# Feed-forward part of a two-block network: the up projection by seven products for eight, the convolution added up in PSUM, the output projection by halves of the tokens

## The chip, the core and the metric

The kernel runs on one core of a Trainium2 chip. The metric is device time in microseconds (us) from the first to the last instruction; a smaller one is better. The engines named below are TensorE (PE in the profile), VectorE (DVE), ScalarE (ACT), GpSimd (POOL) and SyncE (SP, which issues most of the loads and stores). Each works through its own instructions in order; a semaphore holds an instruction, and all behind it on its engine, until what it needs is there.

## What is computed

Two blocks in a row on 1024 tokens of 1024 features. The first (gated linear attention and pooled differences) is not touched. Of the second, cut to what matters:

```python
def second_block(x, ...):
    h = rmsnorm_2(x, attn_norm_g)
    ...                                   # o_fox, o_sb: two kinds of attention, 8 heads each
    o = concatenate([rmsnorm_2(o_fox, fox_out_g), rmsnorm_2(o_sb, sb_out_g)])   # 512 + 512 features
    x = x + o @ w_out                     # output projection, 1024 x 1024
    h = rmsnorm_2(x, ffn_norm_g)
    u = causal_dwconv(h @ w_up, conv_w, conv_b)   # w_up: 1024 x 5632; 3 taps over the tokens, per feature
    gate, val = split(u, 2)               # 2816 features each: 22 tiles of 128
    x = x + (silu(gate) * val) @ w_down   # w_down: 2816 x 1024
    return rmsnorm_2(x, final_norm_g)
```

All is float32 to the caller. A product is made of three float32r matmuls (`mm3`): each operand is split into a high and a low part, and hi·lo, lo·hi and hi·hi are added up in PSUM.

## The kernel before

Activations lie with the features on the 128 partitions and the tokens along the row: `x2` is eight tiles of 128 x 1024. A bank of PSUM holds 128 x 512 values, so each tile of a product's output takes two banks, one for each half of the tokens (`XH`). A weight tile of 128 x 512 (four blocks of 128 features by 128 columns) comes through `load`: one load from memory (256 KB, issued by SP), a cast to the high part on ACT (`whi`), a subtraction for the low part on POOL (`wlo`). There are two buffers for raw weights and four for each part. `tt` (L182) and `stt` (L185) are the helpers for two-operand and scaled two-operand arithmetic, on VectorE unless POOL is named; `split` casts at L190, or at L193 with a scale.

Between the attention and the end, the steps are:

- **Output projection, second half** (from L1105). `out_fox` has made x = xr + (fox half of o) @ w_out while the attention ran (its last additions, `x<-x,t`, are on POOL). What is left is the half of `o_sb`: 8 column tiles (ct) x 2 halves of tokens x 4 features tiles x 3 = 192 matmuls. `gemm_late` takes the first three column tiles: 54 matmuls with the feature tiles 4 to 6, then the norm of `o_sb` (`bank_rstd` at L272, then `rstd`: a multiply-add, Ln, Exp and three more VectorE steps), then the 18 with feature tile 7. The compiler's scheduler, which orders what is ready by priority, puts the 54 between the last steps of the attention. Each result is t = bank * rs, x += t; then the square of x on ACT, its sum `acc` on POOL, and the two parts `u3h`, `u3l` of x * ffg.
- **Up projection.** Column tile 0 is begun by `gemm_late` with the first six feature tiles, before the norm R3 is known. `conv` makes one of the 44 column tiles (22 of gates, 22 of values): 48 matmuls, the two banks times R3, the first tap by ACT (Identity with scale and bias), two taps by `stt`. `up_group` makes two gate and two value tiles, sigmoid and two multiplications, and splits the result into `fh`, `fl` (POOL).
- **Down projection.** After each `up_group`, `down` multiplies the group before by its weights: 11 groups x 96 matmuls, each bank added to `x2`, which stays on the chip. The last group and the final norm go by ranges of tokens (`SEQ`).

PE's matmuls of the feed-forward part: 44 x 48 = 2112 up and 11 x 96 = 1056 down.

## Time and profile before

| | us |
|---|---|
| time, three executions | 2674.43, 2674.55, 2679.32 (median 2674.55) |
| time of the profiled execution | 2679.32 (its span: 2679.3) |
| TensorE busy in the span | 2549.1 (95%) |
| VectorE, ScalarE, GpSimd busy | 1505.9, 961.0, 809.5 |
| from the norm of `o_sb` (1868.2) to the first up matmuls without a gap (1930.5) | 62.3 |
| up and down projections without a gap (1930.5 to 2609.3) | 678.8 |
| the rest, with the last down products and the final norm (2609.3 to 2679.3) | 70.0 |

The profiled execution is the slowest of the three, 4.8 us above the median. Times in the rows count from the start of the span. A row of a stretch gives its length, then the busy time (and the count of instructions) of PE, PEld, DVE, ACT and POOL, the clock that TensorE was granted (1.00 is 2.4 GHz), the share of the DMA engines and GB/s. In a row of the timeline the first number is the start, the second the busy time from there, and the brackets hold the idle time ahead of it with what ended it; `x4` means that neighbours were put together.

### The profile page before, as it was taken

How to read it: one execution, taken by the hardware profiler on the slowest of the kernel's cores; microseconds unless marked ns; L12 is line 12 of the kernel's file. 1: busy time of each engine (PE TensorE's matmuls, PEld its weight loads, DVE VectorE, ACT ScalarE, POOL GpSimd, SP SyncE). 2: the span in 40 equal slices, each digit the busy share in tenths (PEclk: the TensorE clock that was granted, in tenths of full speed). 3: DMA queues.
4: the chain of work that ended last, by engine and by line, in shares of the span. 5: the costliest groups of instructions: out<-in, count | busy, mean ns of one | idle time of the engine just before them, and what ended most of it. 6: DMA issues, size and time to landing. Idle time of an engine off the chain costs nothing. (4 is left out here: it accounts for less than half of the span.)

```text
span 2679.3 us, 36279 instructions
## 1 busy us (share of the span) xinstructions
PE 2549.1 (95%) x14390; PEld 2015.2 (75%) x14390; DVE 1505.9 (56%) x2190; ACT 961.0 (36%) x1634; POOL 809.5 (30%) x592
## 2 busy tenths in 40 slices
PE   6989999999999999999999999999899999999996
PEld 3878977777787888876777766666688888888885
DVE  6363292765927223255766677788934444444456
ACT  4342262553734412332333443433422222222233
POOL 1432221221212224434233222233433333333334
PEclk9989999999999999999999999999999999999998
DMA  6423242433424553335444323430111111111112
GB/s 256 125 74 108 86 158 85 151 111 101 145 80 146 196 193 110 118 103 155 127 127 127 113 77 114 124 105 28 40 49 49 48 48 48 47 48 48 48 48 75
DMA packets 109113, 270.55 MB, mean 101 GB/s; under 512 B 13600, under 2 KB 18592, under 8 KB 108944
## 3 DMA queue, kind: packets, MB, share of 16 engines
q1 hardware_dynamic: 101648, 244.90, 28.3%
q0 software_dynamic: 7296, 23.34, 3.7%
q8 instruction: 113, 1.85, 0.3%
q14 instruction: 56, 0.46, 0.1%
HBM read 192.40 MB, written 71.57 MB: 99 GB/s over the span
## 5 line engine op out<-in xcount | busy, mean ns | idle before, releaser
L182 POOL TENSOR_TENSOR wlo<-wraw,whi 128x512 fp32r<-128x512 f32 (+1 forms) x363 | 537.3, 1482 | 1639.2 <-ACT whi L190 1593.1
L190 ACT CAST whi<-wraw 128x512 fp32r<-128x512 f32 (+1 forms) x363 | 223.8, 617 | 709.4 <-PE pp L238 617.6
L236 PE MATMUL pp<-hl,whi 128*128 128x512 f32 (+1 forms) x768 | 312.1, 407 | 4.8 <-DVE hl L185 4.8
L237 PE MATMUL pp<-hh,wlo 128*128 128x512 f32 (+1 forms) x768 | 307.2, 400 | 0.4 <-POOL wlo L182 0.4
L238 PE MATMUL pp<-hh,whi 128*128 128x512 f32 (+1 forms) x768 | 306.4, 399 | 0.0
L238 PE MATMUL pp<-u3h,whi 128*128 128x512 f32 x688 | 271.4, 395 | 0.0
L237 PE MATMUL pp<-u3h,wlo 128*128 128x512 f32 x688 | 271.0, 394 | 0.0
L236 PE MATMUL pp<-u3l,whi 128*128 128x512 f32 x688 | 270.2, 393 | 0.0
L182 DVE TENSOR_TENSOR x<-x,pp 128x512 f32<-128x512 f32 (+1 forms) x184 | 121.5, 664 | 208.5 <-PE pp L238 208.5
L236 PEld LDWEIGHTS pp<-hl,whi 128*128 128x128 f32 (+1 forms) x768 | 144.9, 189 | 42.5 <-DVE hl L185 5.8
L237 PEld LDWEIGHTS pp<-hh,wlo 128*128 128x128 f32 (+1 forms) x768 | 144.8, 189 | 38.9 <-issue 6.1
L238 PEld LDWEIGHTS pp<-hh,whi 128*128 128x128 f32 (+1 forms) x768 | 144.9, 189 | 33.7 <-issue 0.4
L1028 DVE COPY pt<-pg 128x512 f32<-128x512 f32 (+2 forms) x192 | 101.0, 553 | 92.5 <-PE pg L1026 91.8
L237 PEld LDWEIGHTS pp<-u3h,wlo 128*128 128x128 f32 x688 | 129.0, 188 | 30.9
L236 PEld LDWEIGHTS pp<-u3l,whi 128*128 128x128 f32 x688 | 129.2, 188 | 30.3
L238 PEld LDWEIGHTS pp<-u3h,whi 128*128 128x128 f32 x688 | 129.1, 188 | 30.1
L236 PE MATMUL pp<-fl,whi 128*128 128x512 f32 (+1 forms) x368 | 142.0, 386 | 0.0
L238 PE MATMUL pp<-fh,whi 128*128 128x512 f32 (+1 forms) x368 | 141.4, 384 | 0.0
L237 PE MATMUL pp<-fh,wlo 128*128 128x512 f32 (+1 forms) x368 | 140.8, 383 | 0.0
L185 DVE SCALAR_TENSOR_TENSOR t<-p,vec,t 128x1023 f32<-128x1023 f32 x88 | 122.1, 1395 | 33.1 <-ACT t L1144 32.1
L237 PE MATMUL pp<-uh,wlo 128*128 128x512 f32 x336 | 139.2, 414 | 0.0
L236 PE MATMUL pp<-ul,whi 128*128 128x512 f32 x336 | 138.3, 412 | 0.0
(384 smaller groups left out, 5434.0 us busy)
## 6 DMA issues: line engine op xcount, KB each, us to landing
wraw<-in_w_up SPq DMA_DIRECT2D x88, 256.0 KB
wraw<-in_w_qk SPq DMA_DIRECT2D x48, 256.0 KB
wm<-in_w_mod SPq DMA_DIRECT2D x24, 512.0 KB
wraw<-in_w_dn SPq DMA_DIRECT2D x44, 256.0 KB
x<-in_xT SPq DMA_DIRECT2D x16, 512.0 KB
wraw<-in_w_v SPq DMA_DIRECT2D x32, 256.0 KB
wraw<-in_w_out SPq DMA_DIRECT2D x32, 256.0 KB
q<-qs_d POOLq DMA_DIRECT2D x16, 512.0 KB, 5.0
```

The costliest lines, as they stand in the source:

```text
L182: return (eng or nc.vector).tensor_tensor(out=o, in0=a, in1=b, op=op)
L185: return (eng or nc.vector).scalar_tensor_tensor(out=o, in0=a, scalar=s, in1=b, op0=op0, op1=op1)
L190: nc.scalar.copy(hi, src)
L236: nc.tensor.matmul(ps, ah, bl, start=first, stop=False)
L237: nc.tensor.matmul(ps, al, bh, start=False, stop=False)
L238: nc.tensor.matmul(ps, ah, bh, start=False, stop=last)
L1028: nc.vector.tensor_copy(o, ps[:, :w])
```

## The change

Line numbers after the change are 8 to 20 higher (`tt` L190, `stt` L193, `split`'s cast L199, loads and stores L202, `mm3` L254 to L256).

1. From the output projection to the end of the up projection every instruction is kept in the program's order on its engine (`pinned`).
2. The output projection goes by halves of the tokens, A = 512 to 1023 first, then B = 0 to 511. Each half of x is written to memory (`x2_d`) and read back before the down projection.
3. The up projection takes seven products in place of eight. With w = [[a11, a12], [a21, a22]] for a gate tile and a value tile (rows: the pair (gate, value); columns: the two halves of the features), and the four quarters of h = x * ffg * R3 (two halves of the features, two of the tokens), seven sums of weights meet seven sums of quarters: 22 pairs x 7 products x 4 x 3 = 1848 matmuls. `t_norm` scales a quarter, `t_sum` forms a sum of quarters in place of x, `t_parts` splits it into the 28 tiles `T`; `up_sum` forms four sums of weights per pair on VectorE; `up_parts` splits seven weights per pair. `up_result` puts the products together: two copies on ACT, the other sums on VectorE.
4. The convolution's first tap goes to PSUM (`cv`), and the two others are added there; the sigmoid and the multiplication read it there. The gated result is stored (`f_d`).
5. The down projection runs after the whole up projection, from memory (`gated`), with its 1056 matmuls and the same last part.

```diff
+SEVEN = (1, 6, 2, 5, 7, 3, 4)
+EARLY = (1, 2, 5, 7, 6, 3, 4)
...
-    rs["sb"] = b1k("rs")
-    first = gemm_late(
-        [[load(io["w_out2"][ct, 1], 4, P)] for ct in range(3)], oh, ol, range(4, 8), TAGS[:3], 3,
-        lambda: bank_rstd(acc_o["sb"], rs["sb"], 1.0 / 512, "pg"),
-    )
...
+    get = psum_pool(es, pp=(HALF, 4), cv=(L, 2))
+    pinned[0] = True
...
+    def out_result(ct, half, ps):
+        x, t = x2[ct][:, half], ht("t")
+        tt(t, ps, rs["sb"][:, half], ALU.mult)
+        tt(x, x, t, ALU.add)
+        dma(x2_d[ct][:, half], x)
...
+    def t_norm(k, half):
+        x = quarter(k, half)
+        stt(x, x, V("ffg", k), R3[:, half], ALU.mult, ALU.mult)
+    def t_sum(n, j):
+        o, a, b = {
+            5: ((j, A), (j, B), (j, A)), 7: ((j, B), (j + 4, B), (j, B)),
+            6: ((j + 4, B), (j + 4, B), (j, A)), 4: ((j + 4, A), (j + 4, A), (j + 4, B)),
+        }[n]
+        tt(quarter(*o), quarter(*a), quarter(*b), ALU.subtract)
+    def t_parts(n, j):
+        src = quarter(*{1: (j, A), 2: (j + 4, A), 3: (j + 4, B), 5: (j, A), 7: (j, B), 6: (j + 4, B), 4: (j + 4, A)}[n])
+        t = b1k("T", F32R)
+        split(src, t[:, :HALF], t[:, HALF:], nc.gpsimd if j % 2 else None)
+        T[n].append((t[:, :HALF], t[:, HALF:]))
...
+    def up_sum(q, n):
+        if q >= NFF or (q, n) in sums:
+            return
+        a11, a12, a21, a22 = raws[q]
+        if n in (5, 6):
+            r = ctile("S")
+            sums[q, 5], sums[q, 6] = r[:, :HALF], r[:, HALF:]
+            tt(sums[q, 5], a21, a22, ALU.add)
+            tt(sums[q, 6], sums[q, 5], a11, ALU.subtract)
+        elif n == 3:
+            sums[q, 3] = sums[q, 6]
+            tt(sums[q, 3], a12, sums[q, 6], ALU.subtract)
+        elif n == 7:
+            tt(a11, a11, a21, ALU.subtract)
+            sums[q, 7] = a11
+        else:
+            sums[q, n] = raws[q][{1: 0, 2: 1, 4: 3}[n]]
...
+    def up_product(q, n):
+        wh, wl = wparts.pop((q, n))
+        key = {1: 1, 2: 1, 7: 7, 4: 7}.get(n, 6)
+        new = (q, key) not in banks
+        if new:
+            banks[q, key] = get("pp")
+        ps = banks[q, n] = banks[q, key]
+        for j in range(4):
+            th, tl = T[n][j]
+            mm3(ps, wh[:, j], wl[:, j], th, tl, new and j == 0, j == 3, True)
...
+    def up_result(q, n):
+        b = banks[q, n]
+        p1, u = part.get((q, 1)), part.get((q, "u"))
+        if n == 1:
+            part[q, 1] = ht("p1")
+            copy(part[q, 1], b)
+        elif n == 2:
+            copy(out_row(q, 0)[:, A], b)
+        elif n == 3:
+            tt(out_row(q, 0)[:, B], p1, b, ALU.add)
+        elif n == 4:
+            tt(out_row(q, 1)[:, A], u, b, ALU.add)
+        elif q > 1 and n == 6:
+            part[q, "u"] = ht("u")
+            tt(part[q, "u"], p1, b, ALU.add)
+        elif q > 1 and n == 5:
+            tt(out_row(q, 1)[:, B], p1, b, ALU.add)
+        elif n == 5:
+            part[q, "u"] = ht("u")
+            copy(part[q, "u"], b)
+        elif n == 6:
+            v = out_row(q, 1)[:, B]
+            tt(v, p1, b, ALU.add)
+            tt(u, v, u, ALU.subtract)
+            tt(v, v, banks[q, 7], ALU.add)
+        elif q > 1:
+            v = out_row(q, 1)[:, B]
+            tt(v, v, b, ALU.add)
...
+    def up_rest(q, i):
+        if i == 0:
+            conv_first(q, 0)
+        elif i == 1:
+            conv_first(q, 1)
+            conv_tap(q, 0, 1)
+        elif i == 2:
+            conv_tap(q, 0, 2)
+        elif i == 3:
+            g = act(outs[q, 0], cv[q, 0], AF.Sigmoid)
+            if q == NFF - 1:
+                log_exp_table(g)
+            conv_tap(q, 1, 1)
+        elif i == 4:
+            conv_tap(q, 1, 2)
+        elif i == 5:
+            tt(outs[q, 0], outs[q, 0], cv[q, 0], ALU.mult)
+        else:
+            tt(outs[q, 0], outs[q, 0], cv[q, 1], ALU.mult)
+            dma(f_d[q], outs[q, 0])
...
+    three = [out_load(ct) for ct in range(3)]
+    wide = get("cv")
+    bank3 = [[get("pp"), get("pp")], [get("pp"), get("pp")], [wide[:, :HALF], wide[:, HALF:]]]
+    for w, bs in zip(three, bank3):
+        for b, half in zip(bs, (A, B)):
+            out_product(b, w, half, range(3))
+    wide = get("cv")
+    for half in (A, B):
+        half_rstd(acc_o["sb"], half, wide[:, half], rs["sb"], 1.0 / 512)
+    for i, half in enumerate((A, B)):
+        for ct in range(3):
+            out_product(bank3[ct][i], three[ct], half, (3,))
+    for i, half in enumerate((A, B)):
+        for ct in range(3):
+            out_result(ct, half, bank3[ct][i])
+    todo = [(ct, half) for half in (A, B) for ct in range(3, KD)]
+    ws = [out_load(ct) for ct, _ in todo[:2]]
+    total = None
+    for n, (ct, half) in enumerate(todo):
+        ps = get("pp")
+        out_product(ps, ws[n], half, range(4))
+        if n + 2 < len(todo):
+            ws.append(out_load(todo[n + 2][0]))
+        out_result(ct, half, ps)
+        if n == 4:
+            total = get("cv")
+            half_rstd(acc, A, total[:, A], R3, 1.0 / D)
+            for q in range(2):
+                up_load(q)
+        elif n > 5:
+            for k in (2 * (n - 6), 2 * (n - 6) + 1):
+                t_norm(k, A)
+                t_parts(1 + k // 4, k % 4)
+    order = [(q, n) for n in EARLY for q in range(2)] + [(q, n) for q in range(2, NFF) for n in SEVEN]
+    for q, n in order[:3]:
+        up_parts(q, n)
+    prep = {
+        1: [(t_norm, j, B) for j in range(4)] + [(t_sum, 5, j) for j in range(4)], 2: [(t_parts, 5, j) for j in range(4)],
+        3: [(t_norm, j + 4, B) for j in range(4)] + [(t_sum, 7, j) for j in range(4)], 4: [(t_parts, 7, j) for j in range(4)],
+        5: [(t_parts, 3, j) for j in range(4)], 6: [f for j in range(4) for f in ((t_sum, 6, j), (t_parts, 6, j))],
+        7: [f for j in range(2) for f in ((t_sum, 4, j), (t_parts, 4, j))],
+        8: [f for j in range(2, 4) for f in ((t_sum, 4, j), (t_parts, 4, j))],
+    }
+    for s, (q, n) in enumerate(order):
+        i = s % 7
+        if s == 1:
+            half_rstd(acc, B, total[:, B], R3, 1.0 / D)
+        if s:
+            up_result(*order[s - 1])
+        for f, *a in prep.get(s, ()):
+            f(*a)
+        if s == 8:
+            up_load(2)
+        elif q > 1 and i == 0 and q + 1 < NFF:
+            up_load(q + 1)
+        if i == 3 and s > 7:
+            up_sum(q + 1 if q > 1 else 2, 6)
+        if s + 4 < len(order):
+            up_sum(*order[s + 4])
+        if s + 3 < len(order):
+            up_parts(*order[s + 3])
+        if q > 2:
+            up_rest(q - 1, i)
+        elif s >= 13:
+            for i_ in ((0, 1), (2, 3), (4, 5), (6,))[(s - 13) % 4]:
+                up_rest((s - 13) // 4, i_)
+        up_product(q, n)
+    up_result(*order[-1])
+    for i in range(7):
+        up_rest(NFF - 1, i)
+    pinned[0] = False
...
+    def gated(grp):
+        return unzip([load_split(f_d[2 * grp + kk], lo=nc.gpsimd) for kk in range(2)])
...
-    f = up_group(0)
+    f = gated(0)
+    for ct in range(KD):
+        x2[ct] = b1k("x2")
+        nc.sync.dma_start(x2[ct], x2_d[ct])
     for grp in range(NFF // 2 - 1):
-        nf = up_group(grp + 1)
+        nf = gated(grp + 1)
         for c2 in range(4):
             down(grp, load_down(grp, c2), c2, *f)
```

What the change moves, at three places (rows in the order in which they stand on an engine; `out<-in` with the buffers' numbers; `_16193` and the like are numbers, `pp`, `lg`, `pg`, `cv` banks of PSUM).

**TensorE and GpSimd, end of the attention.** `ol`, `oh` are the parts of `o_sb`, `sm` and `pt` the attention's weights, `whi`, `wlo` the parts of a weight tile. TensorE before:

```order
L952 MATMUL lg_16120<-k_2815_15498,q_2814_15497 128x256
L953 MATMUL lg_16120<-k_2816_15499,q_2814_15497 128x256
L236 MATMUL pp_16209<-ol_14098,whi_16192 128x512
L237 MATMUL pp_16209<-oh_14097,wlo_16193 128x512
L238 MATMUL pp_16209<-oh_14097,whi_16192 128x512
L236 MATMUL pp_16209<-ol_14777,whi_16192 128x512
L237 MATMUL pp_16209<-oh_14776,wlo_16193 128x512
L238 MATMUL pp_16209<-oh_14776,whi_16192 128x512
L236 MATMUL pp_16209<-ol_15491,whi_16192 128x512
L237 MATMUL pp_16209<-oh_15490,wlo_16193 128x512
L238 MATMUL pp_16209<-oh_15490,whi_16192 128x512
L236 MATMUL lg_16211<-ol_14098,whi_16198 128x512
```

TensorE after:

```order
L1057 MATMUL pg_16085<-pt_16078,vt_15524 64x128 x2
L1046 MATMUL pg_16147<-ident,sm_16141 128x128
L1046 MATMUL pg_16161<-ident,sm_16155 128x128 x2
L1057 MATMUL pg_16165<-pt_16146,vt_15524 64x128
L1057 MATMUL pg_16165<-pt_16160,vt_15524 64x128 x2
L254 MATMUL pp_16246<-ol_14128,whi_16228 128x512
L255 MATMUL pp_16246<-oh_14127,wlo_16229 128x512
L256 MATMUL pp_16246<-oh_14127,whi_16228 128x512
```

GpSimd before, at the same place:

```order
L182 TENSOR_TENSOR wlo_16205<-wraw_16203,whi_16204 128x512
L182 TENSOR_TENSOR x_2916_15942<-x_2916_15942,t_15943 128x512 x2
L182 TENSOR_TENSOR wlo_16345<-wraw_16343,whi_16344 128x512
L182 TENSOR_TENSOR x_2943_16066<-x_2943_16066,t_16067 128x512 x2
L182 TENSOR_TENSOR x_2965_16149<-x_2965_16149,t_16150 128x512 x2
L182 TENSOR_TENSOR wlo_16389<-wraw_16387,whi_16388 128x512
```

GpSimd after:

```order
L190 TENSOR_TENSOR x_2916_15972<-x_2916_15972,t_15973 128x512 x2
L190 TENSOR_TENSOR x_2943_16096<-x_2943_16096,t_16097 128x512 x2
L190 TENSOR_TENSOR x_2965_16179<-x_2965_16179,t_16180 128x512 x2
L190 TENSOR_TENSOR wlo_16229<-wraw_16227,whi_16228 128x512
L190 TENSOR_TENSOR wlo_16235<-wraw_16233,whi_16234 128x512
L190 TENSOR_TENSOR wlo_16241<-wraw_16239,whi_16240 128x512
```

The first 54 matmuls of the output projection no longer stand between the attention's steps but behind the last of them (`pg<-pt,vt`), and the low parts of their weights stand behind all additions `x<-x,t` of `out_fox`.

**SyncE, output projection.** `wraw<-in_w_out` is a load of weights, `xr` a load of the residual, `x_d<-x` a store of half a tile of x. Before:

```order
L231 DMA wraw_16197<-in_w_out 128x512
L231 DMA wraw_16203<-in_w_out 128x512
L1089 DMA xr_15941<-x_d_173 128x1024
L231 DMA wraw_16343<-in_w_out 128x512
L1089 DMA xr_16065<-x_d_174 128x1024
L231 DMA wraw_16387<-in_w_out 128x512
L1089 DMA xr_16148<-x_d_175 128x1024
L231 DMA wraw_16431<-in_w_out 128x512
L231 DMA wraw_16475<-in_w_out 128x512
```

After:

```order
L202 DMA wraw_16227<-in_w_out 128x512
L202 DMA wraw_16233<-in_w_out 128x512
L202 DMA wraw_16239<-in_w_out 128x512
L202 DMA x_d_176<-x_2764_15298 128x512
L202 DMA x_d_177<-x_2794_15431 128x512
L202 DMA x_d_178<-x_2829_15570 128x512
L202 DMA x_d_176<-x_2764_15298 128x512
L202 DMA x_d_177<-x_2794_15431 128x512
L202 DMA x_d_178<-x_2829_15570 128x512
L202 DMA wraw_16379<-in_w_out 128x512
L202 DMA wraw_16385<-in_w_out 128x512
```

The fourth and all later loads of weights stand behind the six stores of x, each of which waits for its result.

**VectorE, start of the up projection.** Before, the results of a column tile (`p` is a bank times R3, `t` the convolved tile):

```order
L182 TENSOR_TENSOR p_17323<-pp_17337,R_3051_16562 128x512
L182 TENSOR_TENSOR p_17323<-pp_17363,R_3051_16562 128x512
L185 SCALAR_TENSOR_TENSOR t_17324<-p_17323,vec,t_17324 128x1023
L185 SCALAR_TENSOR_TENSOR t_17324<-p_17323,vec,t_17324 128x1022
L182 TENSOR_TENSOR p_17392<-pp_17406,R_3051_16562 128x512
L182 TENSOR_TENSOR t_17324<-t_17324,sgf_17461 128x1024
L182 TENSOR_TENSOR p_17392<-pp_17432,R_3051_16562 128x512
```

After, the last of the sums and low parts of quarters of h (`x` is the quarter's tile, `T` its parts, `S` a sum of weights), up to the first result that frees a bank for the third pair (`o_16795<-p_3092_16734,pp_16840`):

```order
L190 TENSOR_TENSOR x_2943_16096<-x_2943_16096 128x512
L190 TENSOR_TENSOR T_16947<-x_2943_16096,T_16947 128x512
L190 TENSOR_TENSOR x_2965_16179<-x_2965_16179 128x512
L190 TENSOR_TENSOR o_16976<-p_3092_16734,pp_16840 128x512
L190 TENSOR_TENSOR u_16853<-o_16976,u_16853 128x512
L190 TENSOR_TENSOR o_16976<-o_16976,pp_16907 128x512
L190 TENSOR_TENSOR o_16996<-p_3097_16764,pp_16871 128x512
L190 TENSOR_TENSOR u_16884<-o_16996,u_16884 128x512
L190 TENSOR_TENSOR o_16996<-o_16996,pp_16933 128x512
L190 TENSOR_TENSOR S_17000<-w_16957 128x512
L190 TENSOR_TENSOR S_17000<-S_17000,w_16954 128x512
L190 TENSOR_TENSOR o_16795<-p_3092_16734,pp_16840 128x512
```

From the norm R3 of half B to that result 49 instructions of this kind stand in a row (and 19 subtractions on GpSimd beside them); before, the parts of h were made between the results of the output projection, and only results stood here.

## Rows read from the trace of the kernel before

**Rows 1.** Stretches from the norm of o_sb to the end

```profile
1868.20:1901.70 33.50, 33.50 (x143) 26.45 (x141) 31.83 (x32) 13.91 (x18) 19.07 (x11) 1.00 0.15 40
1901.70:1930.50 28.80, 16.73 (x54) 11.58 (x54) 26.96 (x25) 12.45 (x15) 16.56 (x7) 0.82 0.13 36
1930.50:2609.30 678.80, 678.80 (x2929) 549.58 (x2928) 327.37 (x364) 174.39 (x210) 217.20 (x143) 1.00 0.17 47
2609.30:2679.30 70.00, 49.53 (x261) 41.94 (x259) 46.97 (x76) 25.25 (x47) 29.00 (x25) 0.87 0.22 75
```

**Rows 2.** Timeline, TensorE, end of the attention

```profile
1843.28 0.50 PE L236 MATMUL pp<-ol,whi 128*128 128x512 f32 x1
...
1852.85 1.53 PE L1037 MATMUL pg<-pt,vt 128*64 128x128 f32 x22
...
1867.98 0.39 PE L238 MATMUL lg<-oh,whi 128*128 128x512 f32 x1
1868.21 1.88 PE L272 MATMUL pg<-acc_o,ones 128*128 128x512 f32 x4
```

**Rows 3.** Timeline, VectorE, the attention's last copies

```profile
1850.32 1.02 DVE L1028 COPY pt<-pg 128x512 f32<-128x512 f32 x2
```

**Rows 4.** Timeline, GpSimd, the last additions of out_fox

```profile
1870.34 2.55 POOL L182 TENSOR_TENSOR x<-x,t 128x512 f32<-128x512 f32 x2 [15.22 <-DVE x L185]
```

**Rows 5.** Timeline, TensorE, first up matmuls after a wait

```profile
1905.55 0.47 PE L236 MATMUL lg<-u3l,whi 128*128 128x512 f32 x1 [3.71 <-DVE t L182]
...
1907.04 0.63 PE L236 MATMUL lg<-u3l,whi 128*128 128x512 f32 x1
1907.46 0.63 PE L237 MATMUL lg<-u3h,wlo 128*128 128x512 f32 x1
```

**Rows 6.** Groups by form, VectorE, 1876.7 to 1925.6: busy, mean, idle ahead

```profile
L182 DVE TENSOR_TENSOR x<-x,t 128x512 f32<-128x512 f32 x16 | 22.5, 1432 | 0.1
L185 DVE SCALAR_TENSOR_TENSOR u3l<-x,vec,u3h 128x1024 fp32r<-128x1024 f32 x8 | 14.4, 1797 | 0.2 <-ACT u3h L193 0.2
L182 DVE TENSOR_TENSOR t<-lg,rs 128x512 f32<-128x512 f32 x8 | 5.3, 677 | 0.0
```

**Rows 7.** Groups by form, GpSimd, the same stretch

```profile
L182 POOL TENSOR_TENSOR acc<-acc,sq 128x1024 f32<-128x1024 f32 x6 | 16.5, 2743 | 14.9 <-ACT sq L1122 14.7
L182 POOL TENSOR_TENSOR wlo<-wraw,whi 128x512 fp32r<-128x512 f32 x7 | 13.4, 1912 | 5.8 <-ACT whi L190 5.8
```

**Rows 8.** Timeline, VectorE, the norm R3

```profile
1926.46 0.69 DVE L213 TENSOR_SCALAR rv<-pg 128x512 f32<-128x512 f32 x1 [0.97 <-PE pg L272]
...
1928.51 0.69 DVE L182 TENSOR_TENSOR rt<-R 128x512 f32<-128x512 f32 x1
...
1929.96 0.69 DVE L182 TENSOR_TENSOR rt<-R 128x512 f32<-128x512 f32 x1
1930.57 0.68 DVE L185 SCALAR_TENSOR_TENSOR R<-rt,R 128x512 f32<-128x512 f32 x1
```

**Rows 9.** Timeline, ScalarE, a cast of output weights

```profile
1877.29 0.62 ACT L190 CAST whi<-wraw 128x512 fp32r<-128x512 f32 x1 [3.02 <-DMA wraw<-in_w_out]
```

**Rows 10.** Timeline, SyncE's queue, the load of those weights

```profile
1874.62 2.03 SPq L231 DMA_DIRECT2D wraw<-in_w_out  x2
```

**Rows 11.** Groups by form, VectorE, 1930 to 2609, up and down

```profile
L182 DVE TENSOR_TENSOR x<-x,pp 128x512 f32<-128x512 f32 x144 | 99.0, 688 | 194.9 <-PE pp L238 194.9
L185 DVE SCALAR_TENSOR_TENSOR t<-p,vec,t 128x1023 f32<-128x1023 f32 x43 | 61.2, 1422 | 32.2 <-ACT t L1144 32.1
L185 DVE SCALAR_TENSOR_TENSOR t<-p,vec,t 128x1022 f32<-128x1022 f32 x43 | 59.1, 1374 | 0.9
...
L182 DVE TENSOR_TENSOR t<-t,t 128x1024 f32<-128x1024 f32 x21 | 25.7, 1225 | 0.7
```

**Rows 12.** The page, rate of transfers in 40 equal slices of the span

```profile
GB/s 256 125 74 108 86 158 85 151 111 101 145 80 146 196 193 110 118 103 155 127 127 127 113 77 114 124 105 28 40 49 49 48 48 48 47 48 48 48 48 75
```

More of the change, by code (lines that the diff above doesn't have):

```diff
@@ L1105, in fused_blocks @@
     log_exp_table(state["sig"])
[L1106 to L1117 removed]
+    es.close()
@@ new lines, in fused_blocks, with half_rstd, out_product @@
+    es = ExitStack()
+    get = psum_pool(es, pp=(HALF, 4), cv=(L, 2))
+    pinned[0] = True
+    A, B = slice(HALF, L), slice(0, HALF)
+    rs["sb"], acc, R3 = b1k("rs"), b1k("acc3"), b1k("R3")
+    def half_rstd(src, half, ps, r, scale):
+        pin(nc.tensor.matmul(ps, ones, src[:, half], start=True, stop=True))
+        rstd(ps, r[:, half], HALF, scale)
+    def out_product(bank, w, half, ks):
+        for k in ks:
+            hi, lo = w
+            mm3(bank, hi[:, k], lo[:, k], oh[4 + k][:, half], ol[4 + k][:, half], k == 0, k == 3)
@@ new lines, in up_parts @@
+    def up_parts(q, n):
+        up_sum(q, n)
+        wh = wpool.tile([P, HALF], F32R, tag="whi", bufs=NW, name=f"whi{uid()}")
+        wl = wpool.tile([P, HALF], F32R, tag="wlo", bufs=NW, name=f"wlo{uid()}")
+        split(sums[q, n], wh, wl, nc.gpsimd)
+        wparts[q, n] = [x.rearrange("p (k c) -> p k c", k=4) for x in (wh, wl)]
+    banks, outs, part = {}, {}, {}
+    def up_product(q, n):
[8 more added lines that the diff above has]
+            mm3(ps, wh[:, j], wl[:, j], th, tl, new and j == 0, j == 3, True)
```

125 lines of the change are left out of this document (55 added, 70 removed).

## The prediction

> **What bounds the kernel now.** I read the stretches first, then the timeline of TensorE around each gap, then the engine that ended the gap. From 1930.5 to 2609.3 TensorE is busy for all of 678.80 us at full clock [rows 1]: the up and down projections are bound by TensorE alone, at 678.8 / 2928 = 0.2318 us a matmul. VectorE is busy for 327.37 us of it, and stands idle for 194.9 us before its additions `x<-x,pp` [rows 1, 11]. So each matmul taken out there is worth its 0.2318 us, as long as VectorE stays the faster. Before that stretch it is the other way round: of the 28.8 us from 1901.7 TensorE works 16.73 and VectorE 26.96 [rows 1]; VectorE, which forms x and the parts of h, is what ends last. In the attention's tail the first 54 matmuls of the output projection fill gaps: the first starts at 1843.28, the last at 1867.98, and the norm of `o_sb` follows at 1868.21 [rows 2]. The profiled execution is its span, 2679.3 us; I work on its clock and take 4.8 us off for the median, 2674.55.
>
> **What is saved.** 2112 - 1848 = 264 matmuls x 0.2318 = 61.2 us. The waits of before from 1868.2 to 1930.5 go too: 62.3 us less 186 matmuls x 0.2315 (43.1) leaves 19.2. What follows is the way TensorE's work now takes, as a chain of times.
>
> **1. The 54 matmuls behind the attention.** The attention's last steps lose the matmuls between them (one delay: the copies end at 1851.34, their products start at 1852.85 [rows 2, 3], some 1.5 us). The first low part of the weights now stands on GpSimd behind the last two additions, which ended at 1870.34 + 2.55 = 1872.89 [rows 4]; each half of 512 values costs GpSimd 1.28, so the part is there at 1874.2. TensorE has then been idle, and at the last such start its matmuls fell to half clock for a while (from 1907.04 on, 0.63 us busy and 0.42 apart [rows 5]); eight like these cost 8 x 0.2 = 1.5. I let this stand against the 1.5 of the shorter tail. 1874.2 + 54 x 0.2318 = 1886.7, which I take as 1886.5; before, it was 1868.2: **+18.3**.
>
> **2. The fourth weight tile.** Norm (1.3 us, 1868.21 to 1869.5 before) and 18 matmuls (4.2): 1892.0 on TensorE. But the next loads stand on SyncE behind six stores, the last of which waits for the x of the sixth result. VectorE starts at about 1887.3: two norms of four instructions (8 x 0.61, the pitch of 512 values [rows 8]), two waits for Ln and Exp (rv ends at 1927.15, the next step starts at 1928.51: 1.4 [rows 8]), 15 instructions of results (9.2), three waits for a square (0.7 each, a step of ScalarE like [rows 9] and a hop): 19.0, so 1906.3. Then load to cast 2.67 (1874.62 to 1877.29 [rows 9, 10]), cast 0.6, low part 1.3: 1910.9. TensorE waits 1892.0 to 1910.9: **+18.9**. Behind the waiting store stand all later loads of output weights.
>
> **3. Ten products of 12 matmuls.** At TensorE's pace 27.8 us. Each waits on the chain store, load, cast, low part two products back, some 3.1 us; five give 1926.4. Then eight loads of up weights stand before the load of the eighth product. They follow the store of the fifth result (six VectorE instructions, 3.7): 1930.1; at 256 KB for about 1.0 us each (the fastest slice of the page, 256 GB/s [rows 12]) 1938.1, own load 2.67, cast and part 1.9: 1942.8; three products 8.3, and 0.9 for the last weight, whose cast stands behind parts of h: 1952. **+13.3** against 27.8. The load could hide only if up weights came later.
>
> **4. Start of the up projection.** This is the largest term, and VectorE sets it. During the last four products it has 24 instructions (x, square sums, the scaling and low parts of half A): 14.6, eight waits for ScalarE's casts and squares at 0.65 (5.2), and waits beside GpSimd's six parts (7.8 us). The price of these I take from 1876.7 to 1925.6: there the 16 `x<-x,t`, with both operands in SBUF, took 1.432 against 0.677 for `t<-lg,rs`, which reads a bank, and 8 `u3l` took 1.797 against 1.225 for 1024 values undisturbed [rows 6, 11]: 12.1 + 4.6 = 16.7 us lost. GpSimd worked 6 x 2 + 7 = 19 halves x 1.28 = 24.3 us there [rows 4, 7]. So VectorE loses 0.7 us per us of GpSimd's work: 5.5 here. From 1941.2: 1966.5; then cast, GpSimd's part of T and of the weight (0.6 + 1.3 + 1.3): first up product at 1969.7. The norm of half B follows its product and half of the next (1973.8), and takes 4.9 (1926.46 to 1931.2, with the hop before [rows 8]): 1978.7. From there to the result that frees a bank for the first product of the third pair stand 49 VectorE instructions: 29.9, waits for ScalarE 3.3, and beside them 19 parts on GpSimd (24.7 us x 0.7 = 17.3): 2029.2. TensorE does 14 products (38.9) in the 77.2 from 1952: **+38.3**.
>
> The Trainium skill (SBUF — State Buffer, section "Who interferes with whom") has a rule on these waits: a VectorE instruction with two inputs in SBUF and a GpSimd instruction that reads SBUF share a port, and the later one waits for the whole of the other. It agrees with [rows 6] in which instructions suffer; by it the share would be 1.0 in place of 0.7, and the sum 9.7 us more.
>
> **5. The steady part.** Per pair 84 matmuls, 19.47 us. VectorE: five sums with a bank and four without, 9 x 0.62; four taps at 1.28, two multiplications at 1.22 [rows 11]: 13.1, and at most 4 x 1.3 of waits beside GpSimd: under 18.3. ScalarE and GpSimd have some 9 each (seven parts x 1.28). The taps of before (1.422 and 1.374 [rows 11]) had two inputs in SBUF; the new ones have one in PSUM, which no row shows. I take 1.28, between 1.2 and 1.7. The cost is nothing as long as the step fits. 2029.2 + 140 products x 2.78 (389.5) = 2418.7.
>
> **6. The end.** From up to down the pool of banks changes: four are free at once, 16 matmuls each worth 1.4; I take +1.5 (0 to 6, if a bank of the convolution must be waited for, two taps and two multiplications). Down: 9 groups x 96 x 0.2318 = 200.3, its loads of gated rows at 2.78 a product hidden behind 22 us a group; then 70.0 unchanged [rows 1]. The stores and reloads of x lie beside it, at 47 GB/s of traffic now [rows 1]. 2418.7 + 1.5 + 200.3 + 70.0 = 2690.5 on the profiled clock.
>
> As a sum: -61.2 - 19.2 + 18.3 + 18.9 + 13.3 + 38.3 + 1.5 and 1.3, the second of the two norms between them = +11.2. Median 2674.55 + 11.2 = **2686**, by 0.4% slower.
>
> **The rivals.** (a) *GpSimd hardly disturbs VectorE.* The sum holds 22.8 us for it (5.5 + 17.3). Half of the parts stand on GpSimd so that the two work at once; the waits seen might come of the 1024-wide squares, and the subtractions of 512 may fall between VectorE's. At a share of 0.1 the time is 2686 - 19.5 = 2666; it decides, to faster by over 0.2%, below a share of 0.19. Against it: the `x<-x,t` that lost most are 512 wide themselves [rows 6]. (b) *A middle share*, 0.19 to 0.52: 2669 to 2680, no difference to be told; about 2674. (c) *VectorE bounds the steady part.* If the taps in PSUM and the sums with a bank take longer by 0.35 us for each of six instructions, and each of four subtractions of GpSimd costs its whole 1.3 us, VectorE has 20.4 us a pair against 19.47; some 1 us x 20 pairs gives 2706. It decides from 19.47 us a pair. For it: a result is always issued ahead of the next product and its bank is one of four; against it: the six lie well below on the rows. (That the change does not do what it says is excluded: the order shows 264 matmuls fewer.)
>
> The Trainium skill (Perfetto Trace Analysis, section "Optimizing Scalar/DVE Operations") bears on (c): it gives VectorE an overhead of about 60 ns per access to SBUF and 125 to PSUM. By that six instructions would cost an estimated 0.4 us a pair more, within the slack; [rows 6, 11] do not show it: 677 and 688 ns with a bank.
>
> **How the numbers follow.** Forecast 0.50 (its own range 2680 to 2698: the share from 0.52 to 1.0, and the 0 to 6 of the change of banks); (a) 0.22; (b) 0.17; (c) 0.11. A difference of 0.2% (5.3 us) is about what a measurement can tell. So faster is (a), 0.22; same is (b), 0.17; slower the forecast and (c), 0.61. The range reaches from the lower side of (a), 2661, to (c), 2706.
>
> **What would show it.** Right: a gap on TensorE ahead of the first output matmul to about 1874, a second of some 19 us after 72 of them, ended by a weight's load; VectorE without a gap from 1979 to 2029, its 512-wide additions near 1.0 us or above beside GpSimd; TensorE without gaps from there. Wrong: VectorE's subtractions at 0.7 us beside GpSimd (a), gaps of TensorE in every pair, released by VectorE (c), or weights that come without the wait for the stores.

## The result, and the profile after

The changed kernel took 2703.32 us (median of four executions, 2702.5 to 2704.9) against 2674.49: the ratio is 1.0106, with a 95% interval from 1.0092 to 1.012. It is slower, by 28.8 us, where 11.5 were forecast: the sign is right, the size is less than half of what came. The profiled execution has a span of 2701.5 us and a time of 2703.25; in the later runs of the kernel before, too, the time lies some 1.75 above the span, so that the span of its median is about 2672.7, 6.6 below that of the profile shown ahead of the prediction. Executions also differ in the unchanged first part: some 190 us ahead of the attention's end the same instruction stands 7.7 us earlier in the profile of after than in that of before. Times are therefore compared below from the attention's last product on (`pg<-pt,vt`; it ends at 1864.95 before, at 1855.4 after).

The kernel after by stretches (length, then busy time and count of TensorE, its weight loads, VectorE, ScalarE and GpSimd, granted clock, share of the DMA engines, GB/s):

```profile
1855.40:1885.60 30.20, 21.02 (x76) 15.52 (x76) 6.98 (x8) 6.56 (x11) 6.21 (x5) 0.79 0.03 9
1885.60:1904.50 18.90, 0.16 (x1) 0.00 (x0) 12.59 (x19) 4.62 (x8) 0.00 (x0) 0.59 0.31 111
1904.50:1963.70 59.20, 37.76 (x122) 26.65 (x122) 37.21 (x48) 18.13 (x31) 19.08 (x14) 0.79 0.43 142
1963.70:2031.10 67.40, 49.63 (x171) 36.60 (x171) 52.53 (x57) 26.98 (x46) 43.34 (x28) 0.85 0.05 16
2031.10:2421.70 390.60, 389.43 (x1681) 315.25 (x1679) 286.29 (x304) 174.87 (x246) 192.11 (x142) 1.00 0.24 83
2421.70:2428.90 7.20, 0.20 (x1) 0.00 (x0) 6.86 (x7) 4.84 (x5) 1.40 (x2) 0.71 1.02 359
2428.90:2701.50 272.60, 252.12 (x1124) 206.38 (x1124) 141.89 (x216) 62.42 (x99) 120.31 (x80) 0.96 0.31 99
```

Two of these rows answer to the long one of [rows 1]: from 2031.1 to 2421.7 TensorE works 389.43 of 390.6 us, and from 2428.9 on the down projection runs as before. So the seven products do save their 61 us. Nearly all that is lost stands in the first four rows and the sixth: 176 us from the attention's last product to the steady part, in which TensorE is busy for 109, and 7 us between up and down.

The same places on the timeline of TensorE (start, busy, what ended the idle time ahead):

```profile
1864.59 0.79 PE L255 MATMUL pp<-oh,wlo 128*128 128x512 f32 x1 [5.15 <-POOL wlo L190]
...
1904.55 0.80 PE L254 MATMUL pp<-ol,whi 128*128 128x512 f32 x1 [18.79 <-ACT whi L199]
...
1963.73 0.79 PE L254 MATMUL pp<-T,whi 128*128 128x512 f32 x1 [10.11 <-ACT whi L199]
1966.24 0.79 PE L255 MATMUL pp<-T,wlo 128*128 128x512 f32 x1 [1.71 <-POOL wlo L190]
...
1970.96 1.02 PE L1136 MATMUL cv<-acc,ones 128*128 128x512 f32 x2
...
2019.85 0.47 PE L254 MATMUL pp<-T,whi 128*128 128x512 f32 x1 [2.99 <-ACT T L199]
...
2038.01 0.50 PE L254 MATMUL pp<-T,whi 128*128 128x512 f32 x1 [1.17 <-ACT p L199]
...
2428.93 0.76 PE L254 MATMUL pp<-rl,whi 128*128 128x512 f32 x1 [7.03 <-DVE o L190]
```

The first is the low part behind the additions of `out_fox`: the forecast had TensorE go on 9.3 us behind the attention's end, and it went on at 9.2. The second is the weights behind the stores: 18.9 us were forecast, and 18.8 came. SyncE's queue and ScalarE show the second: six stores as their x come, then the loads, then the cast.

```profile
1889.35 11.17 SPq L202 DMA_DIRECT2D x_d<-x  x6
1900.62 5.58 SPq L202 DMA_DIRECT2D wraw<-in_w_out  x3
```

```profile
1903.88 1.25 ACT L199 CAST whi<-wraw 128x512 fp32r<-128x512 f32 x2 [2.98 <-DMA wraw<-in_w_out]
```

In the steady part VectorE has slack (groups by form, 2100 to 2400):

```profile
L193 DVE SCALAR_TENSOR_TENSOR cv<-o,vec,cv 128x1022 f32<-128x1022 f32 x31 | 39.7, 1280 | 0.0
L193 DVE SCALAR_TENSOR_TENSOR cv<-o,vec,cv 128x1023 f32<-128x1023 f32 x31 | 39.6, 1279 | 0.0
...
L190 DVE TENSOR_TENSOR o<-p,pp 128x512 f32<-128x512 f32 x32 | 22.0, 688 | 32.5 <-PE pp L256 32.5
```

A tap in PSUM takes 1.28 us, the value that had to be chosen without a row, and less than the 1.42 and 1.37 of [rows 11]; the sums with a bank take 688 ns, and it is VectorE that waits for TensorE (32.5 us of idle time ahead of these 32 sums).

### The profile page after: what moved, and what is told of

Same layout as the page of the kernel before. It is cut to its first block, busy times and chain, and to the rows that moved or that the text cites. A ratio compares the mean times of both kernels' runs of the same rounds, so it can differ in the third digit from the quotient of the medians.

```text
span 2701.5 us, 36571 instructions
## 1 busy us (share of the span) xinstructions
PE 2507.0 (93%) x14126; PEld 1975.9 (73%) x14126; DVE 1614.9 (60%) x2351; ACT 1028.7 (38%) x1779; POOL 903.6 (33%) x671
## 5 line engine op out<-in xcount | busy, mean ns | idle before, releaser
L190 POOL TENSOR_TENSOR wlo<-wraw,whi 128x512 fp32r<-128x512 f32 (+1 forms) x280 | 414.5, 1483 | 1376.9 <-ACT whi L199 1321.6
L199 ACT CAST whi<-wraw 128x512 fp32r<-128x512 f32 (+1 forms) x280 | 172.2, 616 | 511.3 <-PE pp L256 380.7
L254 PE MATMUL pp<-hl,whi 128*128 128x512 f32 (+1 forms) x768 | 311.7, 406 | 4.4 <-DVE hl L193 4.4
L256 PE MATMUL pp<-hh,whi 128*128 128x512 f32 (+1 forms) x768 | 305.9, 398 | 0.0
L254 PE MATMUL pp<-rl,whi 128*128 128x512 f32 (+1 forms) x688 | 269.8, 392 | 7.0 <-DVE o L190 7.0
L254 PE MATMUL pp<-T,whi 128*128 128x512 f32 x616 | 246.8, 401 | 26.8 <-ACT whi L199 10.1
L256 PE MATMUL pp<-rh,whi 128*128 128x512 f32 (+1 forms) x688 | 269.7, 392 | 0.0
L255 PE MATMUL pp<-rh,wlo 128*128 128x512 f32 (+1 forms) x688 | 268.9, 391 | 0.0
L255 PE MATMUL pp<-T,wlo 128*128 128x512 f32 x616 | 246.1, 400 | 2.2 <-POOL wlo L190 2.2
L256 PE MATMUL pp<-T,whi 128*128 128x512 f32 x616 | 244.6, 397 | 0.0
L190 DVE TENSOR_TENSOR x<-x,pp 128x512 f32<-128x512 f32 (+1 forms) x184 | 121.7, 664 | 121.2 <-PE pp L256 121.2
L254 PEld LDWEIGHTS pp<-hl,whi 128*128 128x128 f32 (+1 forms) x768 | 144.7, 188 | 42.0 <-DVE hl L193 5.3
L256 PEld LDWEIGHTS pp<-hh,whi 128*128 128x128 f32 (+1 forms) x768 | 144.6, 188 | 33.5 <-issue 0.4
L254 PEld LDWEIGHTS pp<-T,whi 128*128 128x128 f32 x616 | 117.3, 190 | 58.9 <-DVE T L190 11.6
L254 PEld LDWEIGHTS pp<-rl,whi 128*128 128x128 f32 x688 | 130.1, 189 | 37.1 <-issue 9.3
L190 POOL TENSOR_TENSOR wlo<-w,whi 128x512 fp32r<-128x512 f32 x88 | 115.9, 1319 | 122.4 <-ACT whi L199 122.3
L256 PEld LDWEIGHTS pp<-rh,whi 128*128 128x128 f32 x688 | 130.0, 189 | 29.5 <-issue 1.7
L255 PEld LDWEIGHTS pp<-rh,wlo 128*128 128x128 f32 x688 | 130.0, 189 | 29.5 <-issue 1.3
L255 PEld LDWEIGHTS pp<-T,wlo 128*128 128x128 f32 x616 | 117.5, 191 | 30.5 <-POOL wlo L190 3.4
```

The lines of the kernel that those rows point to most:

```text
L190: return pin((eng or nc.vector).tensor_tensor(out=o, in0=a, in1=b, op=op))
L199: return pin(nc.scalar.copy(o, x))
L254: pin(nc.tensor.matmul(ps, ah, bl, start=first, stop=False, skip_group_check=again))
L255: pin(nc.tensor.matmul(ps, al, bh, start=False, stop=False, skip_group_check=again))
L256: pin(nc.tensor.matmul(ps, ah, bh, start=False, stop=last, skip_group_check=again))
```

## The experiments

All are edits of the changed kernel. Where whole times are compared, the executions' spread counts (up to 13 us between the lowest and the highest of one kernel), and beside these runs the kernel before took 2675.7 to 2676.4 us in the median. The profile's way from the attention's last product to the end is steadier, and is given first: it is 846.1 us in the changed kernel and 814.4 in the kernel before. Each kernel has one profile, and parts of the way that an edit does not touch differ by up to 1.3 us between them; the down projection does so because behind the same wait of 7.0 us now 7, now 13 of its matmuls take 0.6 us in place of 0.39.

**Loads ahead of the stores.**

```diff
+    ws = [out_load(ct) for ct, _ in todo[:2]]
     for i, half in enumerate((A, B)):
         for ct in range(3):
             out_result(ct, half, bank3[ct][i])
-    ws = [out_load(ct) for ct, _ in todo[:2]]
...
-        dma(x2_d[ct][:, half], x)
+        held.append((x2_d[ct][:, half], x))
...
             ws.append(out_load(todo[n + 2][0]))
+        store_held()
         out_result(ct, half, ps)
```

> Of the changed kernel, one thing altered: the loads of the fourth and later weight tiles of the output projection are issued ahead of the stores of x, no longer behind them. The theory (these stores hold the loads, and with them the chain that ends last): TensorE's wait of 18.8 us before the ten products falls to 3 or less, VectorE's idle 8.7 us behind the sixth result goes, and each of the ten products is released from a store: 9 to 15 us less than 2703, so 2688 to 2694. The rival (VectorE's own queue sets the end, and the wait only moves to the products behind): 2701 to 2705.

Measured: 834.0 us from the attention's end, 12.1 less; time 2696.9 (two executions, 2694.7 and 2699.1). The first of the ten products begins 35.3 us behind the attention in place of 49.2, and now waits for a bank:

```profile
1894.20 0.77 PE L254 MATMUL pp<-ol,whi 128*128 128x512 f32 x1 [4.88 <-DVE t L190]
```

The wait of 18.8 is 4.9, a little above the 3 that were expected, since the first product now meets the results of VectorE; the gain along the chain is as the theory had it (11.0 of the 12.1 are there at the third pair, the rest is the spread of the down projection), though the two times lie 1 to 5 us above what it gave. The stores did hold the loads.

**The 54 products among the attention.**

```diff
-    es.close()
-    es = ExitStack()
-    get = psum_pool(es, pp=(HALF, 4), cv=(L, 2))
-    pinned[0] = True
...
-    bank3 = [[get("pp"), get("pp")], [get("pp"), get("pp")], [wide[:, :HALF], wide[:, HALF:]]]
+    bank3 = [[get("pp"), get("pp")], [get("lg"), get("lg")], [get("lg"), get("lg")]]
...
+    pinned[0] = True
     for half in (A, B):
-        half_rstd(acc_o["sb"], half, wide[:, half], rs["sb"], 1.0 / 512)
+        half_rstd(acc_o["sb"], half, get("pg"), rs["sb"], 1.0 / 512)
...
+    es.close()
+    es = ExitStack()
+    get = psum_pool(es, pp=(HALF, 4), cv=(L, 2))
     total = None
```

> Of the changed kernel, one thing altered: the first 54 matmuls of the output projection and the loads and parts of their weights are not kept in the program's order and use banks of the attention's pool, so that they stand between the last steps of the attention as in the kernel before. The theory (term 1 of the prediction is real, 54 matmuls late are about 17 us on the path, and all behind moves with them): 2703 less 15 to 18, 2685 to 2688, with the 18.8 us wait for weights unchanged. The rival (the attention's tail, which was shorter without them, takes most of it back): 2695 to 2703.

Measured: 826.5 us from the attention's end, 19.6 less; time 2687.8, within the theory's range. The last of the 54 stands 3.0 us behind the attention's end, 23.0 in the changed kernel, and the attention itself takes no longer with the products in it: its last 186 us are 186.0 against 185.9. So the rival falls. The wait for weights was to stay at 18.8 and is 2.3 longer:

```profile
1889.39 0.80 PE L254 MATMUL pp<-ol,whi 128*128 128x512 f32 x1 [21.05 <-ACT whi L199]
```

The gain is 20.0 us at the last of the 54 and 17.1 at the first up product; the theory holds, and 54 products late are worth some 17 us. The other 2.4 of the 19.6 arose from the change from up to down on: with the banks of this edit TensorE does six down matmuls before it waits, and then waits 5.5 us in place of 7.0.

**The up projection's banks kept for the down projection.**

```diff
-    es.close()
-    es = ExitStack()
-    get = psum_pool(es, pp=(HALF, 8))
```

> Of the changed kernel, one thing altered: the down projection goes on with the four banks of the up projection; the pool of eight is not opened. The theory (TensorE's wait of 7.0 us between up and down is for a bank that the last pair's convolution still reads, and costs some 1.5 us of low clock besides): 7 to 9 us less than 2703, 2694 to 2697, with no wait there above 1.5 us. The rival (the wait is for the gated rows or the weights, or four banks are too few for the down products, whose results wait for VectorE): 2700 or more.

Measured: 835.9 us from the attention's end, 10.2 less; time 2698.2. The wait is gone; the first down matmul follows the last up matmul at TensorE's pace:

```profile
2423.76 0.40 PE L256 MATMUL pp<-T,whi 128*128 128x512 f32 x1
2424.00 0.39 PE L254 MATMUL pp<-rl,whi 128*128 128x512 f32 x1
```

Of the 10.2, the wait gave 7.2 and the way from there to the end 1.9 (270.7 for 272.6); the other 1.1 arose ahead of it, in a part that the edit does not touch, and is spread. The time lies between the two expectations. In the changed kernel the wait ended during the last two multiplications of the last pair, when the first of them, which reads a bank of the convolution, was done:

```profile
2427.57 2.47 DVE L190 TENSOR_TENSOR o<-o,cv 128x1024 f32<-128x1024 f32 x2
```

So the first bank that the new pool hands out is taken to be that bank of the convolution; with the old pool kept there is no such wait.

**No GpSimd beside VectorE.** In the start of the up projection ScalarE makes a second copy where GpSimd made the low part, so these low parts are left out.

```diff
-        split(src, t[:, :HALF], t[:, HALF:], nc.gpsimd if j % 2 else None)
+        if half_copied[0] and j % 2:
+            copy(t[:, :HALF], src)
+            copy(t[:, HALF:], src)
+        else:
+            split(src, t[:, :HALF], t[:, HALF:], nc.gpsimd if j % 2 else None)
...
-        split(sums[q, n], wh, wl, nc.gpsimd)
+        if half_copied[0] and q < 3:
+            copy(wh, sums[q, n])
+            copy(wl, sums[q, n])
+        else:
+            split(sums[q, n], wh, wl, nc.gpsimd)
```

> Of the changed kernel, at the start of the up projection (half of the 28 tiles of parts, and the weights of the first three pairs) the low part is a copy by ScalarE in place of the subtraction by GpSimd, so these low parts are left out as such. The theory (VectorE loses 0.7 us for each us that GpSimd works beside it, some 17 us from the norm of half B to the first result that lets TensorE go on): that stretch of VectorE falls from 50 to 35 us, its 512-wide sums from 1.0 to 0.65 us in the mean, and the time to 2686 to 2693. The rival (VectorE waits for ScalarE and for its own operands, not for GpSimd): the sums keep their mean, and ScalarE's 40 further copies make it 2700 to 2710.

Measured: 834.0 us from the attention's end, 12.1 less; time 2696.4, 3 above the expected. VectorE's stretch from the norm R3 of half B to the first result of product 3 falls from 50.2 to 40.2 us. Groups by form in that stretch, the changed kernel first, then this one:

```profile
L190 DVE TENSOR_TENSOR T<-x,T 128x512 fp32r<-128x512 f32 x10 | 14.1, 1436 | 2.9 <-ACT T L199 2.9
L190 DVE TENSOR_TENSOR x<-x 128x512 f32<-128x512 f32 x8 | 7.4, 950 | 0.0
```

```profile
L190 DVE TENSOR_TENSOR T<-x,T 128x512 fp32r<-128x512 f32 x10 | 6.7, 690 | 8.8 <-ACT T L199 8.8
...
L190 DVE TENSOR_TENSOR x<-x 128x512 f32<-128x512 f32 x8 | 5.2, 687 | 0.0
```

Both groups fall to 0.69 us. With 49 instructions at 0.61 (29.9) and 3.6 us of idle time, 16.7 us had been lost beside 20 parts on GpSimd of 1.28 each (25.6): a share of 0.65, where 0.7 had been taken. Here 40.2 - 29.9 - 9.1 of idle time leaves 1.2. The stretch did not fall to 35 because ScalarE's further copies made VectorE wait 8.8 us in place of 2.9. And 3.7 of the 10 us do not reach TensorE: the third pair begins 7.4 us behind this stretch, 3.7 in the changed kernel.

How the loss comes about stands in the timeline of the changed kernel. Of the instructions of VectorE with both operands in SBUF, 19 begin beside a part of GpSimd in this stretch, and 18 of them end 0.55 us after that part does. The parts are longer too: 17 of the 20 take 1.57 to 1.76 us in place of 1.28. One of each, and two reads of a bank that stand beside parts as well:

```profile
2016.86 1.71 POOL L190 TENSOR_TENSOR wlo<-S,whi 128x512 fp32r<-128x512 f32 x1
...
2022.82 5.16 POOL L190 TENSOR_TENSOR wlo<-w,whi 128x512 fp32r<-128x512 f32 x3
```

```profile
2017.37 1.74 DVE L190 TENSOR_TENSOR x<-x 128x512 f32<-128x512 f32 x1
...
2026.73 1.27 DVE L190 TENSOR_TENSOR o<-p,pp 128x512 f32<-128x512 f32 x2
```

So VectorE waits until the part has ended, while the reads of a bank keep their pitch (two in 1.27). The 18 waits make up the 16.7 us, some 0.93 each; a part of 1.28 costs less than its length because it mostly begins while VectorE is still at work.

**All low parts of h on VectorE.**

```diff
-        split(src, t[:, :HALF], t[:, HALF:], nc.gpsimd if j % 2 else None)
+        split(src, t[:, :HALF], t[:, HALF:], None)
```

> Of the changed kernel, one thing altered: the low parts of all 28 tiles of h's sums are made by VectorE, none by GpSimd, which keeps those of the weights. 14 subtractions move. The theory (each us of GpSimd costs VectorE some 0.6 to 0.7 us beside it): a subtraction costs VectorE 0.61 itself and spares 0.8 to 0.9 of waiting, and GpSimd's own 1.3 us leave the way of the weights' parts: 2 to 6 us less than 2703, 2697 to 2701, with VectorE's sums nearer 0.7 us. The rival (the waits are mostly beside the weights, or VectorE's number of instructions is what counts): 14 x 0.61 = 8.5 us more, 2708 to 2712.

Measured: 850.1 us from the attention's end, 4.0 more; time 2711.7. Neither expectation held. The same stretch now has 59 instructions and lasts 50.6 us: 36.0 at the pitch, 6.3 idle, 8.3 lost beside ten parts (12.8 us on GpSimd, again 0.65). Its group answers to the two above:

```profile
L190 DVE TENSOR_TENSOR T<-x,T 128x512 fp32r<-128x512 f32 x20 | 14.3, 753 | 6.1 <-ACT T L199 6.1
```

Each moved subtraction costs 0.61 and a further wait of 0.3 for ScalarE's cast, and spares 0.83: nothing is won there. Most of the loss, 3.0 us, is there before the stretch, in half A (first up product 111.3 us behind the attention, 108.3 in the changed kernel).

**The three edits together**, and with the low parts on VectorE.

> The three edits together, the output products among the attention's last steps, the loads of output weights ahead of the stores of x, and the down projection on the up projection's banks. Counted from the attention's last product to the end, the edits alone gave 12, 18 to 20 and 10 us. The theory (three separate waits on one chain): they add up, 38 to 42 less than 2703, 2661 to 2667, and the kernel is faster than before by 0.3%. The rival (they overlap: with the products early the loads are hidden or VectorE's queue takes over): 2668 to 2680, no faster than before.

> The three edits together and the low parts of all tiles of h on VectorE. By the theory of the lost time beside GpSimd 2 to 6 us less than with the three edits alone; by the rival 5 to 9 more.

Measured: the three together 2673.1 us (2668.9 to 2678.5, ten executions), ratio to before 0.9986, interval 0.9974 to 0.9998; 811.3 us from the attention's end, 34.8 less than the changed kernel, where the sum of the three would be 41.9. By time this is the rival's range: they overlap by 7, of which some 2 lie at the change from up to down, where the second and the third edit both gain. The products wait again, now for the last of the six results on VectorE; that the first bank of the new pool is one of those is borne out below, where the results are taken in another order.

```profile
1887.45 0.77 PE L254 MATMUL pp<-ol,whi 128*128 128x512 f32 x1 [18.26 <-DVE t L190]
```

With the low parts on VectorE as well 2677.1 us, 817.8 from the attention's end: 6.5 more, as in the single run a loss.

**Sums behind the next result**, and the six results in the banks' order. In the run of the three edits VectorE stood still at each square, as in this row of its timeline:

```profile
1879.20 0.69 DVE L190 TENSOR_TENSOR acc<-acc,sq 128x512 f32<-128x512 f32 x1 [0.70 <-ACT sq L196]
```

```diff
         tt(x, x, t, ALU.add)
+        add_late()
...
             act(sq, x, AF.Square)
-            tt(acc[:, half], acc[:, half], sq, ALU.add)
+            late.append((half, sq))
...
                 t_norm(k, A)
+            for k in (2 * (n - 6), 2 * (n - 6) + 1):
                 t_parts(1 + k // 4, k % 4)
```

Here `add_late` adds the square of the result before to the sum. The second run has this on top of it:

```diff
-    for i, half in enumerate((A, B)):
-        for ct in range(3):
+    for i, half in ((1, B), (0, A)):
+        for ct in (0, 2, 1):
             out_result(ct, half, bank3[ct][i])
```

> The three edits together, and VectorE's order altered between the output projection and the up projection: the sum of squares of a result stands behind the x of the next result, and the two parts of half A that a product brings stand behind both scalings, so that VectorE does not stand still while ScalarE squares or casts. The theory (from the norm of o_sb on VectorE's queue in order sets the end; 0.70 us were lost at each of 14 squares and 0.69 at each of 4 casts): 7 to 13 us less than the 2673 of the three edits, 2660 to 2666, and below the kernel before by 0.3% or more. The rival (TensorE's products, weights or loads are next in line and take it over): 2668 to 2673.

> As the run with the sums late, and the first six results taken in the order in which the ten products need their banks (half B first, then A; column tiles 0, 2, 1). The theory: TensorE's wait of 18.3 us before the ten products, which then ended with the last of the six results, ends some 9 us earlier and VectorE's gap of 2.65 us behind the sixth result goes: 2 to 4 us less than without it. The rival (half A's sum and norm come later and take it back): the same or up to 3 more.

Measured: 2664.0 us (ratio 0.9957, 0.9942 to 0.9971), 803.3 from the attention's end, 8.0 less; with the results in the banks' order 2659.9 (0.9941, 0.9926 to 0.9956), 801.2, another 2.1. Both came as the theory had them, though 2.1 is little above the spread; at the third pair it is 2.7. The wait ahead of the ten products is 18.3 us with the three edits, 15.2 with the sums late and 8.9 in the second run:

```profile
1879.56 0.77 PE L254 MATMUL pp<-ol,whi 128*128 128x512 f32 x1 [8.93 <-ACT acc L196]
```

The profile names ScalarE's first square, of which the product reads nothing; VectorE's read of a bank ended 0.07 us before that, and its queue, taken in order, is what the products waited for:

```profile
1878.73 0.68 DVE L190 TENSOR_TENSOR t<-lg,rs 128x512 f32<-128x512 f32 x1
```

This version is 0.6% faster than the kernel before, with all 1848 products and the down projection from memory as the change made them.

**Two tiles of the last quarter one step later.**

```diff
-        8: [f for j in range(2, 4) for f in ((t_sum, 4, j), (t_parts, 4, j))],
+        9: [f for j in range(2, 4) for f in ((t_sum, 4, j), (t_parts, 4, j))],
```

> Of the changed kernel, one thing altered: two of the four tiles of the last quarter (two sums, their parts) are made one step later, behind the first read of product 6 of the first pair. The theory (product 3 of a pair adds to the bank of product 6, so TensorE waits for VectorE's read of it, and four products of 2.78 stand between that and the third pair; the prediction had taken a result eight rows further on): the third pair's first product starts 1.5 to 4 us earlier, counted from the attention's last product (175.7 us in the changed kernel). The rival (TensorE waits for the low part of the weights of product 3, or for these tiles): no change within 1 us.

Measured: the third pair's first product stands 179.1 us behind the attention, 3.4 later, where the theory had it earlier and the rival unmoved; time 2707.8. Product 3 of the first pair itself begins 3.0 us earlier (161.5 for 164.5), as the theory wants, and loses 1.25 of it at its second matmul, to the low part of its weights; but then product 3 of the second pair waits, and now by name for VectorE's read of its product 6, ahead of which the moved tiles stand:

```profile
2025.13 0.51 PE L254 MATMUL pp<-T,whi 128*128 128x512 f32 x1 [3.10 <-DVE o L190]
```

So the wait is of the kind that was supposed, and the edit moved it to the next product; the gain that it was to bring did not come, and what the first of these waits costs by itself is not shown.

## Why the prediction was right in sign and wrong in size

From the attention's last product to the end the prediction's chain has 825.5 us, and 846.1 came: 20.6 too few. (The forecast missed by 17.3 in all. The attention's last 186 us ahead of this became some 2 us shorter, which the forecast had set against the low clock of term 1; the rest is the choice of profile and median.) Step by step, the prediction's interval, then what came:

| step | predicted | measured |
|---|---|---|
| attention's end to the 54th product | 21.6 | 23.2 |
| norm and 18 matmuls | 5.5 | 7.0 |
| wait for weights | 18.9 | 18.8 |
| ten products, and wait for the first up product | 58.8 | 59.2 |
| first up product to the norm R3 of half B | 9.0 | 13.5 |
| 49 instructions of VectorE | 50.5 | 50.2 |
| from there to the third pair | 0 | 3.7 |
| 140 products | 389.5 | 390.6 |
| up to down | 1.5 | 7.2 |
| down and the end | 270.3 | 272.6 |

Three steps make up 13.9 of the 20.6: from up to down, which term 6 put at 1.5 and which took 7.2; from the first up product to the norm R3, put at 9.0 and 13.5 long; and from VectorE's result to the third pair, put at nothing, with no reason given, and 3.7 long. The other steps lie within 2.3 us each.

**What was saved** was right: 1848 matmuls at full pace, and the steady part holds. **Terms 1 and 2** were right, and the first two experiments show each by taking it away: some 17 us for the first; 12 for the second, whose 18.9 are not all to be had, since VectorE's results hold the products next. In term 1 the low clock did cost some 1.5 us, and the shorter tail that was set against it came, but ahead of the mark that the table counts from. The norm's second half waited 0.8 us for VectorE's read of a bank.

**Term 3** had the two parts wrong and the sum right: the ten products took 49.1 us for 41.1, because TensorE stood still again and again and ran at half clock after the longer waits (granted clock 0.79), but the first up product came 10.1 us behind them in place of 17.7. TensorE was not on the path there; VectorE was, as the run with the late sums shows.

**Term 4** was right in its largest part: 49 instructions in 50.2 us, with 16.7 for GpSimd where 17.3 had been put. The share is 0.65; the run without GpSimd's parts shows that the loss goes with them, and that with VectorE's own parts gives the share again. The rivals that hung on it, (a) and (b), fall. A step that failed is the one behind it: "to the result that frees a bank for the first product of the third pair". TensorE's order has four products of 2.78 ahead of that pair, and the first of these adds to the bank of product 6, which VectorE reads eight rows earlier (at 2019.04, until 2019.71; product 3 follows at 2019.85; the order shown ahead of the prediction has the same bank, `pp_16840`, in both rows). The profile puts this wait down to a cast of `T`, but the tile cast there belongs to product 4. The forecast let TensorE start at the later row with nothing left to do: 3.7 us too early. What the trace shows here is the order and the times; the run that was to take this wait away moved it.

```profile
2019.04 0.67 DVE L190 TENSOR_TENSOR o<-p,pp 128x512 f32<-128x512 f32 x1
```

The other step that failed in term 4 is the way to the norm of half B: from the first up product to that norm's matmuls 4.1 us were given, and they came after 7.2, with 1.7 of waiting for the low part of the weights and eleven matmuls at 0.43 apart, and the norm took 6.2 in place of 4.9. VectorE stood idle for 8.2 us meanwhile. This is read from the trace of the changed kernel; no run takes it away.

**Term 5 and rival (c).** The steady part is bound by TensorE; a tap costs 1.28 and (c) falls. A single wait of 1.17 us is left at 2038.0, where ScalarE loads a table for the first sigmoid ahead of a copy that frees a bank:

```profile
2035.16 1.28 ACT L196 ACT_TABLE_LOAD   x1 [3.19 <-DVE cv L193]
```

**Term 6** was mis-sized: 1.5 was chosen from 0 to 6, on the thought that the four banks of the products are free at once. But the first down product waits until VectorE has read a bank of the convolution; the wait was 7.0, above the range, and the third experiment takes it away. The clock that fell in it costs most of the 2.3 us that the down projection is longer: 13 of its matmuls take 0.6 us or more, none with the banks kept.

On the rule of the Trainium skill (SBUF — State Buffer, section "Who interferes with whom"): the trace agrees on which instructions wait, since sums with both operands in SBUF fall to 0.69 us when GpSimd does not work beside them, and the taps and sums with one operand in PSUM keep 1.28 and 0.69 all along. It agrees on the blocking too: 18 of 19 such instructions that begin beside a part end 0.55 us behind the part's end. The prediction took the rule to mean a share of 1.0; that does not follow, since a part costs VectorE only the time by which it outlasts the instruction under way, and measured is 0.65. The Trainium skill (Perfetto Trace Analysis, section "Optimizing Scalar/DVE Operations") gives VectorE a larger overhead on PSUM than on SBUF; no run here shows it: 688 ns with a bank, 684 to 692 without.

## What to carry to other kernels

A change that takes matmuls out of a stretch bound by TensorE was paid at its seams here: count for each seam what stands in order ahead of the instruction that lets TensorE go on, on every queue, stores on the load queue among them, and walk on from the result that is read to the products that still stand ahead of the one you care about. Where a scheduler had hoisted work into gaps, keeping the program's order takes that away; here leaving the first products free, loads ahead of stores and the same banks for the next phase gave back all that the change had lost. In a stretch that VectorE sets, put the use of another engine's result one step behind.

## What the runs showed that was not expected

TensorE's clock was low more often than the one place that the prediction allowed for: from 1855 to 2031 the changed kernel ran 72 of its products' 360 matmuls at 0.6 us or more busy in place of 0.39, in stretches with a granted clock of 0.59 to 0.85, each time after TensorE had waited. At 0.2 us each that is an estimated 14 us, most of it beside VectorE's chain; on the chain are those of term 1 and the eleven ahead of the norm of half B. The other point is the spread between executions: the unchanged first part of the program differed by up to 7.7 us between the profiles, more than several of the effects sought, so that ways between two marks of one profile told more than whole times.
